# Weights of the first products moved ahead of the norm, one factor ahead of its weights, and output-projection parts placed step by step, in a two-layer decoder trunk

## The chip, the cores and the metric

The kernel runs on one core of a Trainium2 chip. The metric is the device time of one execution in microseconds. The tensor engine (PE) multiplies; the vector engine (DVE), the scalar engine (ACT) and the GpSimd engine (POOL) do the elementwise work; SP and POOL issue the DMA transfers.

## The reference, cut to what matters

The input x has 512 tokens of 1024 features. Two layers follow each other, all in float32:

```
alpha = (2 * DEPTH) ** 0.25
for l in range(2):
    y = mla(x) if l == 0 else swa(x)         # attention of layer A, attention of layer B
    x = layernorm(alpha * x + y)             # the first norm of the layer
    x = layernorm(alpha * x + relu(x @ w_up) ** 2 @ w_down)
```

Layer A's attention has 8 heads of 128 and ends with a product by w_o (1024 x 1024). Layer B's attention has 16 query heads of 64 over 4 shared key and value heads, looks at a window of 128 tokens with a bias per head, and ends with a product by w_so (1024 x 1024). Each MLP goes from 1024 to 4096 features and back.

## The kernel before, in words

**Two halves for one number.** Every float32 operand is split into a high part (a copy on ACT, names wh, xth, oh, fac) and the rest (a subtraction on DVE or POOL, names wl, xtl, ol). A product is three matmuls: high by high, high by low, low by high. The function split emits the ACT copy and then the subtraction. All loads of weights, copies, subtractions and matmuls stand in a program order that the Python code writes; each engine runs its own instructions in that order, and `pinned`, `behind(...)` and `tc.high_priority()` shift single instructions in it.

**Weights as a stream.** All weights form one list, `stream`. Entry i is loaded by SP into one of two raw buffers (or into a buffer of four quarters, wq), and split into a ring of four pairs wh/wl. `weights(name)` hands out the next pair and, while doing so, prepares later entries, at most `AHEAD = 4` on the ring and none at or past `state["hold"]`. The first four entries of each MLP have tiles of their own off the ring ("aside": w_fac, w_quada, w_quadb, w_a). `holds[l]` says how many of them may be prepared before the first norm of layer l, and `prepare(n)` raises that bound by n after each token tile's norm.

**The MLP as seven products.** The 4096 features are worked off in four blocks. Each block's up product is done with seven products of half size (steps U'1 ... U'7) instead of eight, each of two weights of 1024 columns; the down products (D1 ... D7) likewise. The weights of several products are sums of quarters: SP loads the first quarter into wq, it is split, and then a POOL DMA adds the next quarter onto the same buffer (line L191, `accum_op=ALU.add`), which is split in turn, and so on. `XFactors` makes the factors of the input side for the first block. Its method `rest` makes those of products 6, 7 and 4; it is called at the first U'5, before the matmuls of which both weights are taken by `Block.up`.

**The end of the attention and the first norm.** `TokMajor` is the product by w_o or w_so: token tile t (128 tokens) by quarter kp of the contracted features. `part(t, kp)` does 6 matmuls for the left 512 columns. `finish(gb, dst, early)` does the parts not yet done, takes the four weights of the right columns, calls `load_gb` (two loads on SP, L385 and L386, of the norm's g and b), and then for each token tile runs 24 matmuls, the evacuation (L534 on DVE, x = alpha x + mm), the statistics (L527, L531, L393), and the norm itself (L396, rs on POOL at L377, L400). After tile t it prepares `early[t]` more weights: `(0, 2, 1, 2)`. One tile later PE turns the normed tile around by transposes (L623), and ACT and DVE split the result.

**Layer B's attention.** `run_steps` goes over 16 heads: scores of head u + 2 (8 matmuls, then DVE adds the bias, ACT takes the exponential, POOL scales p at L1232 and L1234), filling work, `turn` of head u (transposes of p, L1245 and L1247), and `mix` of head u - 1 (8 matmuls by the values). Every second head ends an o tile, whose split goes to oh on ACT and ol on POOL. Filling work is a list of (cost, latest step, earliest step, function): queries by halves (`queries(m, part)`, 24 matmuls of 512 columns in two parts, whose result ACT and DVE copy to q at L1188 and L1189), values, and six parts of w_so. An entry runs when the cost spent so far is under its share of the total or its latest step has come, and only if its earliest step has come.

Of the kernel before, what the change touches and what calls it, by code (L numbers as in the profile page):

```python
# [48 lines left out]
def build(tc, nc, io, out):  # L49
    with ExitStack() as top:  # L50
# [61 lines left out]
        stream, off_ring = [], []  # L112
# [14 lines left out]
        def queue(name, ap, low=nc.vector):  # L127


            index = len(stream)  # L130

            def make(pieces=1, between=None):
                cols = ap.shape[-1]
                raw = at_hand.pop(index) if index in at_hand else raw_tile()
                wh, wl = tiles_of_weights()
                for j in range(pieces):
                    c = slice(j * cols // pieces, (j + 1) * cols // pieces)
                    if between:
                        between(j)
                    if index not in fetched:  # L140
                        pe(nc.sync.dma_start(raw[:, c], ap[:, c]))
                    split(wh[:, c], wl[:, c], raw[:, c], low)
                return wh, wl

            def fetch(raw):
                at_hand[index] = raw
                fetched.add(index)
                pe(nc.sync.dma_start(raw[:, : ap.shape[-1]], ap))

            fetchers[index] = fetch  # L150
            stream.append((name, make))
            off_ring.append(False)
# [12 lines left out]
        def queue_seven(name, key, chunk):  # L165

            quads = {}

            def half(a, jp):
                if a not in quads:
                    if (key, a) == ("U", "a"):
                        quads[a] = xp.tile([P, 4, 512], F32, tag="xt", bufs=8, name=nm("wq"))
                    elif (key, a) == ("U", "b"):
                        quads[a] = gp.tile([P, 4, 512], F32, tag="gb", bufs=1, name=nm("wq"))
                    else:
                        quads[a] = mlp_pool[0].tile([P, 4, 512], F32, tag="quad" + a, bufs=1, name=nm("wq"))
                return quads[a][:, 2 * jp : 2 * jp + 2, :]

            def flat(ap):
                return ap.rearrange("p a b -> p (a b)")

            def grown(a, jp, *more, aside=None):
                wh, wl = tiles_of_weights(aside)
                with behind(state.get("s4") if (key, a, jp, bool(more)) == ("U", "b", 0, True) else None):
                    state["last"] = split(
                        wh, wl, flat(half(a, jp)), keep=(a, bool(more)) == ("b", True) and key == "U"
                    )
                if more:  # L190
                    nc.gpsimd.dma_start(half(a, jp), chunk(*more, jp), accum_op=ALU.add)  # L191
                return wh, wl

            def loaded(a, jp, at, *more, aside=None):
                pe(nc.sync.dma_start(half(a, jp), chunk(*at, jp)))
                return grown(a, jp, *more, aside=aside)

            def alone(jp, aside=None):
                raw = raw_tile()
                pe(nc.sync.dma_start(raw.rearrange("p (a b) -> p a b", a=2), chunk(1, 0, jp)))  # L200
                wh, wl = tiles_of_weights(aside)
                split(wh, wl, raw)
                return wh, wl

            of = {
                1: lambda jp, aside=None: loaded("a", jp, (0, 0), 0, 1, aside=aside),
                5: lambda jp: grown("a", jp, 1, 1),
                6: lambda jp: grown("a", jp, 1, 0),
                4: lambda jp: grown("a", jp),
                2: alone,  # L210
                3: lambda jp: loaded("b", jp, (1, 1), 0, 1),
                7: lambda jp: grown("b", jp),
            }

            def add(n, asides=(None, None)):
                for jp, aside in enumerate(asides):
                    make = (lambda jp=jp, aside=aside: of[n](jp, aside)) if aside else (lambda jp=jp: of[n](jp))
                    stream.append((name, make))
                    off_ring.append(aside is not None)

            return add
# [23 lines left out]
        holds = []  # L245

        def mlp_stream(l):
            holds.append(len(stream) + 1)
            def up(q):

                return lambda r, c, jp: io["up"][
                    l, q * 8 + 4 * c + 2 * jp : q * 8 + 4 * c + 2 * jp + 2, :, r * 512 : (r + 1) * 512
                ].rearrange("c p x -> p c x")

            def down(q):
                return lambda r, c, jp: io["down"][l, q * 8 + 4 * c + 2 * (1 - r) + jp].rearrange(
                    "p (a b) -> p a b", a=2
                )

            add = {("U", q): queue_seven("up", "U", up(q)) for q in range(NFF)}  # L260
            add |= {("D", q): queue_seven("down", "D", down(q)) for q in range(NFF - 1)}
            for i, (which, q, n) in enumerate(steps_of()):
                if i < 2:
                    add[which, q](n, [lambda j=2 * i + jp: aside_of(j) for jp in range(2)])
                else:
                    add[which, q](n)
            for c in range(8):
                queue("down", io["down"][l, (NFF - 1) * 8 + c])
# [14 lines left out]
        state = {"next": 0, "at": 0, "hold": 0}  # L283
# [50 lines left out]
        b = bank()  # L334
# [258 lines left out]
        class XFactors(Factors):  # L593
# [49 lines left out]
            def rest(self):  # L643

                a11, _, a21, a22 = [f32(self.xf[i][:, n]) for i in range(2) for n in range(2)]
                with behind(state["last"]):
                    nc.vector.tensor_sub(self.a, self.a, a11)
                    split(self.part(6, 0), self.part(6, 1), self.a)
                    nc.vector.tensor_sub(self.b, a11, a21)
                    split(self.part(7, 0), self.part(7, 1), self.b)  # L650
                    split(self.part(4, 0), self.part(4, 1), a22)

        def mlp(src, gb, dst, mp):
# [17 lines left out]
            class Block:  # L671
# [16 lines left out]
                    return self.g[name]  # L688

                def up(self, n):  # L690
                    w = [weights("up") for _ in range(2)]
                    if (self.q, n) == (0, 5):
                        src.rest()
                    key = {3: 3}.get(n) or own_bank[n]
                    for j in range(4):

                        b = self.bank(("U", key), j // 2)
                        wh, wl = w[j // 2]
                        for k in range(4):
                            c = slice(j % 2 * 512 + k * P, j % 2 * 512 + (k + 1) * P)  # L700
                            group(
                                b[:, j % 2 * 256 : j % 2 * 256 + 256],
                                three(wh[:, c], wl[:, c], src.part(n, 0)[:, k, :], src.part(n, 1)[:, k, :]),
                                n not in (2, 4) and k == 0 and j % 2 == 0, k == 3, skip_group_check=True,
                            )
                        if j % 2:
                            self.up_out(n, j // 2)
                        if (self.q, j) == (0, 1) and n in (1, 2):
                            with tc.high_priority():
                                src.turn(n + 1)  # L710
# [74 lines left out]
            at = {}  # L785
# [19 lines left out]
            gb = gb()  # L805
# [320 lines left out]
        with tc.tile_pool(name="mlp0", bufs=1) as mp:  # L1126
            mlp_pool[0] = mp
            state["hold"] = holds[0]
            x1 = XFactors(mp)
            proj.finish(gb, x1, (0, 2, 1, 2))  # L1130
            mlp(x1, lambda: load_gb(io["ln_mlp_g"][0], io["ln_mlp_b"][0]), x2, mp)

        mlp_pool[0] = None
# [1 line left out]
        with tc.tile_pool(name="swa", bufs=1) as mp:  # L1135
# [145 lines left out]
            for m in range(1, 8):  # L1281
                for part in range(2):
                    fill.append((2.6, 2 * m - AHEAD_B - 3 + part, -9, lambda m=m, part=part: queries(m, part)))
                if m == 1:
                    for t in range(1, NT):
                        fill.append((2.6, 0, -9, lambda t=t: values(t)))
            for t in range(2):
                for kp in range(3):
                    at = 11 if (t, kp) < (0, 2) else (11, 14)[t] + kp
                    fill.append((1.3, 11 if at == 11 else 99, at, lambda t=t, kp=kp: proj.part(t, kp)))  # L1290
            load_bias(0)
            begin(
                x2,
# [7 lines left out]
        with tc.tile_pool(name="mlp1", bufs=1) as mp:  # L1301
            mlp_pool[0] = mp
            state["hold"] = holds[1]
            x3 = XFactors(mp)
            proj.finish(gb, x3, (0, 2, 1, 2))
            mlp(x3, lambda: load_gb(io["ln_mlp_g"][1], io["ln_mlp_b"][1]), None, mp)


# [107 lines left out]
```

## Time and profile before

| | us |
|---|---|
| three runs | 1029.98, 1026.42, 1027.87 |
| median | 1027.87 |
| the profiled execution | 1029.26 |
| its span in the profile | 1027.2 |
| mean granted clock of TensorE over the span | 0.99 |

In the profile's rows a start is counted in microseconds from the beginning of the span, and 2.06 us of the profiled execution lie outside it. The engines' rows show for each instruction its start, its duration, its engine, line, operation and tiles, and in brackets how long the engine sat idle before it and what ended the wait. Matmuls are pipelined, so a matmul's duration (0.39 us at 512 columns) is longer than the step to the next one (0.23 us).

### The profile page before, as it was taken

Reading aid. Unit: us, or ns where it says so; the run is one execution under the profiler, and the core shown is the slowest. Engines: PE = TensorE matmul, PEld = TensorE weight load, DVE = VectorE, ACT = ScalarE, POOL = GpSimd, SP = SyncE. Lnnn points to the kernel's source line nnn. Section 1 sums busy time; section 2 is a strip of 40 time slices with the busy share of each in tenths; the row PEclk is TensorE's granted clock in tenths of the full one; section 3 lists DMA queues with packets and bytes.
Section 4 is the critical chain, followed back from the end, with each engine's and each line's share of the span. In section 5 each row is a group of like instructions: output and inputs, shape, how many; then the busy total and the mean of one; then the engine's idle time right before and its main releaser. Section 6 shows DMA issues by size and latency. Waiting matters only on the chain.

```text
span 1027.2 us, 15878 instructions
## 1 busy us (share of the span) xinstructions
PE 1000.3 (97%) x6148; PEld 897.7 (87%) x6148; DVE 768.4 (75%) x1233; ACT 556.4 (54%) x849; POOL 219.1 (21%) x204
## 2 busy tenths in 40 slices
PE   8999999998999999999999998999899999999997
PEld 7888887997999989998889897889799998998986
DVE  5588856988769769886685578498886796797756
ACT  5456643457537637646146689345664664565620
POOL 0231101212211211210004675112022122122000
PEclk9999999999999999999999999999899999999999
DMA  7431126488877986964132212349777788898432
GB/s 241 142 96 42 62 103 185 105 187 226 157 168 209 184 179 195 229 113 144 62 103 93 83 63 73 104 101 224 199 149 152 181 224 149 202 249 154 92 122 82
DMA packets 60246, 149.55 MB, mean 146 GB/s; under 512 B 5211, under 2 KB 9740, under 8 KB 60172
## 3 DMA queue, kind: packets, MB, share of 16 engines
q0 software_dynamic: 24320, 58.73, 32.0%
q1 hardware_dynamic: 35852, 89.82, 25.8%
q8 instruction: 48, 0.79, 0.3%
q14 instruction: 26, 0.21, 0.1%
HBM read 146.41 MB, written 4.22 MB: 147 GB/s over the span
## 4 chain that ended last, share of the span: by engine, by line
PE 85%; DMA 5%; DVE 4%; ACT 3%; issue 1%; SPq 0%; POOL 0%; DVEq 0%; ACTq 0%; POOLq 0%
PE mm L104 78%; PE tr L104 4%; DMA wq<-in_up 3%; DVE wl L80 1%; ACT wh L77 1%; DMA xraw<-in_xT 1%; DMA gb<-in_ln_mix_b 1%; PE tr L1075 1%; DMA raw<-in_w_o 1%; PE tr L1245 1%; DMA raw<-in_w_v 1%; PE tr L623 1%; ACT a L740 0%; PE tr L1247 0%; DVE x L400 0%
## 5 line engine op out<-in xcount | busy, mean ns | idle before, releaser
L104 PE MATMUL mm<-wh,fac 128*128 128x512 f32 (+1 forms) x944 | 295.6, 390 | 6.4 <-ACT fac L77 4.4
L77 ACT ACTIVATE wh<-wq 128x1024 fp32r<-128x1024 f32 x164 | 173.7, 1060 | 207.4 <-PE mm L104 144.0
L80 DVE TENSOR_TENSOR wl<-wq,wh 128x1024 fp32r<-128x1024 f32 x164 | 199.5, 1221 | 81.1 <-ACT wh L77 80.1
L104 PE MATMUL mm<-xth,wh 128*128 128x256 f32 (+1 forms) x936 | 245.7, 290 | 0.2 <-DVE a L734 0.2
L104 PE MATMUL mm<-xth,wl 128*128 128x256 f32 (+1 forms) x808 | 235.3, 291 | 0.0
L104 PEld LDWEIGHTS mm<-wh,fac 128*128 128x128 f32 x944 | 177.4, 189 | 44.0 <-ACT fac L77 4.8
L104 PE MATMUL mm<-xtl,wh 128*128 128x256 f32 (+1 forms) x680 | 199.6, 293 | 1.2 <-DVE xtl L80 1.2
L104 PE MATMUL mm<-wl,fac 128*128 128x512 f32 (+1 forms) x472 | 183.3, 388 | 0.0
L104 PEld LDWEIGHTS mm<-xth,wh 128*128 128x128 f32 x936 | 170.8, 192 | 3.2 <-issue 0.4
L104 PEld LDWEIGHTS mm<-xth,wl 128*128 128x128 f32 x808 | 155.5, 192 | 2.3
L191 POOL DMA_DIRECT2D wq<-in_up x64 | 77.5, 1223 | 279.6 <-DVE wl L80 205.9
L77 ACT ACTIVATE wh<-raw 128x1024 fp32r<-128x1024 f32 (+4 forms) x85 | 84.8, 998 | 92.7 <-PE mm L104 57.6
L104 PEld LDWEIGHTS mm<-xtl,wh 128*128 128x128 f32 x680 | 131.0, 193 | 4.4 <-DVE xtl L80 1.4
L80 DVE TENSOR_TENSOR wl<-raw,wh 128x1024 fp32r<-128x1024 f32 (+3 forms) x64 | 74.9, 1177 | 48.0 <-ACT wh L77 47.8
L104 PEld LDWEIGHTS mm<-wl,fac 128*128 128x128 f32 x472 | 89.5, 190 | 17.0
L191 POOL DMA_DIRECT2D wq<-in_down x48 | 42.0, 876 | 189.9 <-DVE wl L80 170.0
L80 POOL TENSOR_TENSOR wl<-raw,wh 128x1024 fp32r<-128x1024 f32 (+2 forms) x21 | 43.8, 2090 | 81.2 <-ACT wh L77 81.1
L104 PE MATMUL mm<-wh,ol 128*128 128x512 f32 x128 | 50.9, 398 | 1.8 <-POOL ol L80 1.8
L104 PE MATMUL mm<-wl,oh 128*128 128x512 f32 x128 | 50.6, 396 | 1.0 <-DVE wl L80 0.9
L104 PE MATMUL mm<-wh,oh 128*128 128x512 f32 x128 | 51.4, 402 | 0.2 <-ACT oh L77 0.2
L377 POOL TENSOR_TENSOR rs<-mv,half 128x1 f32<-128x1 f32 x16 | 11.1, 691 | 169.4 <-DVE mv L393 169.4
L537 DVE TENSOR_TENSOR x<-mm,x 128x512 f32<-128x512 f32 (+1 forms) x49 | 32.9, 674 | 14.7 <-PE mm L104 14.6
(217 smaller groups left out, 1845.9 us busy)
## 6 DMA issues: line engine op xcount, KB each, us to landing
wq<-in_up POOLq DMA_DIRECT2D x64, 512.0 KB, 7.7
wq<-in_down POOLq DMA_DIRECT2D x48, 512.0 KB, 6.4
wq<-in_up SPq DMA_DIRECT2D x32, 512.0 KB, 5.3
raw<-in_down SPq DMA_DIRECT2D x28, 512.0 KB, 6.8
wq<-in_down SPq DMA_DIRECT2D x24, 512.0 KB, 7.0
raw<-in_up SPq DMA_DIRECT2D x16, 512.0 KB, 5.6
raw<-in_w_o SPq DMA_DIRECT2D x8, 512.0 KB, 3.8
raw<-in_w_sq SPq DMA_DIRECT2D x8, 512.0 KB, 3.3
```

Of the source, the lines that this page charges most:

```text
L77: high = nc.scalar.activation(dst_h, src, AF.Copy)
L80: low = (engine or nc.vector).tensor_sub(dst_l, src, f32(dst_h))
L104: pe(nc.tensor.matmul(dst, st, mv, start=first and i == 0, stop=last and i == len(pairs) - 1, **kw))
L191: nc.gpsimd.dma_start(half(a, jp), chunk(*more, jp), accum_op=ALU.add)
L377: nc.gpsimd.tensor_tensor(r, v, half, ALU.pow)
L537: nc.vector.tensor_add(xs[t][:, c], b, xs[t][:, c])
L623: pe(nc.tensor.transpose(pt[:, a, :], xs[t][:, k * P : (k + 1) * P], ident))
L1075: pe(nc.tensor.transpose(pt[:, kb * P : (kb + 1) * P], p[:, kb * P : (kb + 1) * P], ident))
L1245: pe(nc.tensor.transpose(pt[:, a, 0:P], p[:, kb, P:256], ident))
```

## The change

Four edits. First, `holds` rises by three, and `early` becomes (0, 0, 0, 2): all four weights kept aside are loaded and split before the first norm, and the loads of g and b come behind theirs on SP. The plain splits of the ring note themselves in `state["plain"]`, and the first split of a weight kept aside is placed behind the last of them. Second, `rest()` is called between the two weights of the first U'5 and no longer after them, and the splits of product 6's second weights and the like are placed behind the instructions that make the factor (`state["s2", jp]`). Third, the six filling entries of w_so become eight, cost nothing in the pacing, and each has one step at which it runs. Fourth, since these entries count no cost, the total that paces the other filling work falls from 52.0 to 44.2.

On every engine the number of instructions stays the same, and so does the number of DMA issues; only their order changes.

```diff
-                    split(wh[:, c], wl[:, c], raw[:, c], low)
+                    state["plain"] = split(wh[:, c], wl[:, c], raw[:, c], low)
...
             def grown(a, jp, *more, aside=None):
                 wh, wl = tiles_of_weights(aside)
-                with behind(state.get("s4") if (key, a, jp, bool(more)) == ("U", "b", 0, True) else None):
+                after = None
+                if aside:
+                    after = state.pop("plain", None)
+                elif (key, a, jp, bool(more)) == ("U", "b", 0, True):
+                    after = state.get("s4")
+                elif (key, a, more) == ("U", "a", (1, 0)):
+                    after = state.pop(("s2", jp), None)
+                with behind(after):
                     state["last"] = split(
...
         def mlp_stream(l):
-            holds.append(len(stream) + 1)
+            holds.append(len(stream) + 4)
...
                 with behind(state["last"]):
-                    nc.vector.tensor_sub(self.a, self.a, a11)
-                    split(self.part(6, 0), self.part(6, 1), self.a)
+                    state["s2", 0] = (nc.vector.tensor_sub(self.a, self.a, a11),)
+                    state["s2", 1] = split(self.part(6, 0), self.part(6, 1), self.a)
...
                 def up(self, n):
-                    w = [weights("up") for _ in range(2)]
+                    w = [weights("up")]
                     if (self.q, n) == (0, 5):
                         src.rest()
+                    w.append(weights("up"))
...
-            proj.finish(gb, x1, (0, 2, 1, 2))
+            proj.finish(gb, x1, (0, 0, 0, 2))
...
-            for t in range(2):
-                for kp in range(3):
-                    at = 11 if (t, kp) < (0, 2) else (11, 14)[t] + kp
-                    fill.append((1.3, 11 if at == 11 else 99, at, lambda t=t, kp=kp: proj.part(t, kp)))
+            for t, kp, u in ((0, 0, 11), (0, 1, 11), (1, 0, 13), (1, 1, 14), (2, 0, 14), (2, 1, 15), (0, 2, 15), (1, 2, 16)):
+                fill.append((0, u, u, lambda t=t, kp=kp: proj.part(t, kp)))
...
-            proj.finish(gb, x3, (0, 2, 1, 2))
+            proj.finish(gb, x3, (0, 0, 0, 2))
```

## The prediction

> **What bounds the kernel now.** I read the page's busy times and chain first, then PE's waits, then the granted clock in stretches, then the timelines of the places that the change touches.
>
> ```profile
> PE 1000.3 (97%) x6148; PEld 897.7 (87%) x6148; DVE 768.4 (75%) x1233; ACT 556.4 (54%) x849; POOL 219.1 (21%) x204
> PE 85%; DMA 5%; DVE 4%; ACT 3%; issue 1%; SPq 0%; POOL 0%; DVEq 0%; ACTq 0%; POOLq 0%
> ```
>
> PE works for 97% of the span and carries 85% of the chain. The work on PE stays the same, so the time can only change by the places where PE waits, old ones that go and new ones that come. The old ones, from PE's waits:
>
> ```profile
> PE mm L104 <- ACT fac L77: 4.4, 2, 2.4
> PE tr L104 <- DVE xtl L80: 2.1, 2, 1.1
> PE mm L104 <- POOL ol L80: 1.8, 1, 1.8
> ```
>
> None is over 2.4 us. But a wait can cost twice, because the granted clock halves after some of them. In the stretches the columns are PE, PEld, DVE, ACT and POOL busy, then the clock:
>
> ```profile
> 214.71:218.12 3.41, 1.50 (x11) 1.10 (x9) 3.10 (x3) 2.80 (x4) 0.99 (x1) 1.00 1.13 207
> 218.12:221.54 3.42, 3.42 (x17) 3.42 (x18) 3.33 (x3) 2.90 (x4) 0.21 (x1) 0.50 1.13 206
> 235.19:238.60 3.41, 1.75 (x15) 1.55 (x13) 2.49 (x3) 3.41 (x4) 0.00 (x0) 1.00 1.05 211
> 238.60:242.01 3.41, 2.36 (x9) 1.66 (x10) 2.97 (x4) 3.24 (x4) 0.00 (x0) 1.00 0.77 210
> 637.96:641.37 3.41, 1.65 (x7) 0.73 (x6) 2.21 (x7) 3.36 (x13) 2.88 (x3) 1.00 0.01 2
> 641.37:644.79 3.42, 3.19 (x8) 2.41 (x9) 0.34 (x2) 0.30 (x3) 2.00 (x3) 0.50 0.00 0
> ```
>
> A stretch of 3.41 us with PE busy for 1.50 or 1.65 us is followed by one at clock 0.50; with 1.75 us busy it is not. So about half a stretch idle (1.71 us) halves the next stretch, which then does 1.7 us less work. Whether a wait falls into one stretch or is divided between two depends on where the stretches lie.
>
> A rule speaks to this. The Trainium skill, "TensorE: Matmul & The Clock Gate", section "Why this matters for your kernels", sees a drop only from idle gaps of about 3 us or more, and "What's actually happening" there has the window free-running at 3413 ns. By it no wait of this kernel, old or new, would halve the clock; the rows disagree (0.50 after waits of 2.3 us in sum), and they decide. The length of the window agrees with the rows.
>
> **Part 1, the weights ahead of the norm, layer A.** DVE, PE, ACT and SP at this place:
>
> ```profile
> 167.53 1.23 DVE L80 TENSOR_TENSOR w_fac<-wq,w_fac 128x1024 fp32r<-128x1024 f32 x1 [1.13 <-ACT w_fac L77]
> 169.93 1.22 DVE L80 TENSOR_TENSOR wl<-raw,wh 128x1024 fp32r<-128x1024 f32 x1
> 172.68 0.69 DVE L534 SCALAR_TENSOR_TENSOR x<-x,mm 128x512 f32<-128x512 f32 x1 [0.76 <-PE mm L104]
> 176.12 1.28 DVE L400 SCALAR_TENSOR_TENSOR x<-x,rs,gb 128x1024 f32<-128x1024 f32 x1 [0.46 <-POOL rs L377]
> 169.87 0.39 PE L104 MATMUL mm<-wh,oh 128*128 128x512 f32 x1
> 171.20 0.50 PE L104 MATMUL mm<-wl,oh 128*128 128x512 f32 x1 [0.94 <-DVE wl L80]
> 177.95 0.60 PE L623 MATMUL tr<-ident,x 128*128 128x128 f32 x4
> 167.40 1.04 ACT L77 ACTIVATE wh<-raw 128x1024 fp32r<-128x1024 f32 x1
> 176.83 1.06 ACT L77 ACTIVATE w_a<-raw 128x1024 fp32r<-128x1024 f32 x1 [3.41 <-DMA raw<-in_up]
> raw<-in_w_o SPq DMA_DIRECT2D x1, 512.0 KB, 3.2
> raw<-in_up SPq DMA_DIRECT2D x1, 512.0 KB, 7.8
> ```
>
> *Removed:* the eighth weight of w_o no longer stands behind w_fac on ACT and DVE. Its ACT copy moves from 167.40 to about 165.9, when the matmuls have freed its ring place, and its DVE half from 169.93 to 167.6. PE's wait for it, 171.20 less 169.87 less a step of 0.23, is 1.10 us, and goes. PE then reaches the first transpose (L623) at 176.85, not 177.95.
>
> *Added, on DVE's queue ahead of the evacuation of tile 0 (172.68):* from wl's end at 168.8 come the statistics of the last tile (about 0.7), then w_fac, w_quada and w_quadb at 1.2 each, to 173.1, and then w_a. The last one binds. Its raw buffer is free only when wl has ended, so SP issues its load at 168.8, and the loads of g and b queue behind that. I take 3.9 us to landing, bounded by 3.2 (a weight load that ran alone) and 7.8 (one that stood behind the loads of g and b, which now come later); nearer to 3.2, since the loads of g and b are no longer ahead. It lands at 172.7; ACT's copy ends at 173.75, DVE's part at 174.9. From evacuation to normed tile take 172.68 to 177.40, 4.7 us: the tile is ready at 179.65. PE stands from 176.85 to 179.7, 2.85 us, net 1.75 more than before. With the load at 3.2 DVE itself binds at 173.1 and the net is 1.1; with 5.6, about halfway, it is 3.4. Behind w_a on ACT nothing is due before tile 0's transposes; behind it on DVE waits tile 0's evacuation, and for that PE. The later tiles move with it and lose w_quada, w_quadb and w_a out of their own stretch. POOL issues its second accumulating load ahead of tile 0's rs now, at about 172.9, and is free before rs is due at 176.6. The loads of g and b, issued at 169.3 and 169.7 instead of 161, are needed at 176.7 and 178.4, 7.4 and 8.7 us later; they are covered at the price of a load in a row, and if not, the tile is late by the same amount.
>
> **Part 2, the sixth factor ahead of its weights,** and what it meets next:
>
> ```profile
> 215.44 0.28 PE L104 MATMUL mm<-xth,wl 128*128 128x256 f32 x1
> 216.57 0.38 PE L104 MATMUL tr<-xth,wh 128*128 128x256 f32 x1 [0.84 <-ACT xth L77]
> 218.02 0.51 PE L104 MATMUL tr<-xtl,wh 128*128 128x256 f32 x1 [1.07 <-DVE xtl L80]
> 715.93 0.39 PE L104 MATMUL tr<-xtl,wh 128*128 128x256 f32 x1 [1.07 <-DVE xtl L80]
> 236.66 0.28 PE L104 MATMUL mm<-xth,wl 128*128 128x256 f32 x1
> 238.93 0.50 PE L104 MATMUL mm<-wh,fac 128*128 128x512 f32 x1 [1.99 <-ACT fac L77]
> 736.20 0.50 PE L104 MATMUL mm<-wh,fac 128*128 128x512 f32 x1 [2.44 <-ACT fac L77]
> ```
>
> The waits are 1.00 + 1.33 = 2.33 us in layer A and 1.33 in layer B (start to start less a step of 0.12). The factor's halves are moved past one weight split, some 1.1 us on ACT and 1.2 on DVE (rows of w_a and wl above), and PE itself comes 1.75 us later out of part 1, while the factor's inputs do not. That is 2.9 us or more against 2.33, so the waits go; without the delay of part 1 about 1.1 us would stay in layer A. What is late next is the first D'1, 238.93. There ACT has a row of copies and squares ahead of fac, fed by the products just before (it is busy for all of 235.19 to 238.60 above). If PE arrives a little earlier, this queue moves with it only as far as the weights' accumulated loads allow. I keep the wait: about 0.2 us of the gain is given back in layer A, and 0.5 us gained in layer B. Ends: nothing given back, or all 2.33.
>
> Layer A so far: -1.10 + 2.85 - 2.33 + 0.2 = -0.4 us.
>
> **Part 3, the filling work of layer B.** The total cost falls from 52.0 to 44.2, so each step's target falls by 15%, and one early entry slips by a step: the 24 matmuls of a value part (128x256) that stood between the scores of head 1 and of head 2 come after both.
>
> ```profile
> 555.71 0.28 PE L104 MATMUL mm<-skl,q 128*128 128x256 f32 x1
> 555.83 0.28 PE L104 MATMUL mm<-wh,xth 128*128 128x256 f32 x1
> 556.96 0.68 DVE L1189 TENSOR_TENSOR q<-mm,q 64x512 fp32r<-64x512 f32 x1
> ```
>
> Head 2's q ends on DVE at 557.64. Before, PE had 24 x 0.12 = 2.9 us of value work from 555.83 on to cover it. Now the scores of head 2, and all PE work behind them, wait: PE stands from 555.83 to 557.69: +1.86 us. The value work comes later and hides nothing, because PE has no later wait nearby. Bounds: 0 if DVE takes q ahead of head 1's bias additions (about 1.4 us of it), 1.9 if not; the order has q behind them, so 1.86.
>
> At the end of the attention:
>
> ```profile
> 634.94 0.38 PE L104 MATMUL mm<-skh,q 128*128 128x256 f32 x1 [0.43 <-DVE o L1275]
> 636.33 0.20 ACT L1225 ACTIVATION_READ_ACCUMULATOR p<-mm,nb 128x1 f32 x1
> 638.85 1.47 POOL L1234 TENSOR_TENSOR p<-p,ri 128x768 f32<-128x768 f32 x1
> 640.28 1.27 POOL L80 TENSOR_TENSOR ol<-o,oh 128x512 fp32r<-128x512 f32 x1
> 641.60 0.80 PE L104 MATMUL mm<-wh,ol 128*128 128x512 f32 x1 [1.80 <-POOL ol L80]
> ```
>
> Between 634.94 and 641.60 PE stands for about 3 us in sum, start to start less the steps; the largest piece is that for ol (1.80 and the restart), which POOL could begin only after a p of 1.47 us. The parts of w_so now lie between the transposes and mixes, and ol is split ahead of that p: these waits go. One comes: the first part that is moved needs a bank that head 14's scores free only when ACT has taken their exponential, at 636.53; PE gets there when the four score steps from 634.94 are done, at about 635.45, and waits about 1.1 us. Net -2.0 us; ends -3.1 (the bank is free) and -1.0.
>
> **Part 4, the front of the norm in layer B.**
>
> ```profile
> 668.81 1.21 DVE L80 TENSOR_TENSOR wl<-raw,wh 128x1024 fp32r<-128x1024 f32 x1
> 674.64 1.28 DVE L400 SCALAR_TENSOR_TENSOR x<-x,rs,gb 128x1024 f32<-128x1024 f32 x1
> 676.79 1.03 PE L623 MATMUL tr<-ident,x 128*128 128x128 f32 x8
> ```
>
> Here the normed tile was ready at 675.92, 0.87 us early, and PE hardly waited for wl (about 0.2). By the sum of part 1 the same edit puts w_a's end 6.0 us behind wl's end, and the tile 10.4 us behind it instead of 5.9: 4.5 later. wl itself comes earlier against PE, as w_fac's ACT copy (1.06) and DVE half (1.23) no longer stand ahead of it; evacuations still do, and I take 1.4 of at most 2.3. So PE waits 4.5 - 0.87 - 1.4 = 2.2 to 2.4, and with the wait for wl gone the net is +2.1 (0.8 with wl at its earliest and the load at 3.2; 4 with the load at 5.6).
>
> Layer B: 1.86 - 2.0 + 2.1 - 1.33 - 0.5 = +0.1 us. Both layers: **-0.3 us** at full clock.
>
> **The clock.** Of the halved stretches the one at 218.12 goes (-1.7), and that at 641.37 with a chance of two thirds (-1.1), as 1.7 us of wait is left there. New waits can halve: a wait of w falls into one stretch with 1.71 us or more at about w/3.41 of the positions. That is 0.85 for 2.85 us, 0.55 for 1.86, 0.7 for 2.35, and some 0.7 for the first D'1 of layer A, which was just above the limit (1.75) and waits a little longer at first. Together 2.8 stretches, 4.8 us. The sum is -0.3 - 2.8 + 4.8 = +1.7 us: 1031.0 against the profiled execution (1029.26). That one lies 1.4 above the median of the runs, and the runs are spread over 3.6 us, two halved stretches; against the median the same sum gives 1029.5. A difference of 0.3%, 3.1 us, is about what a measurement of this kernel can tell from no change.
>
> **The rivals.** (a) *Every new wait halves the clock* and the tail's stays: 4 x 1.7 - 1.7 - 0.3 = +4.8, 1032.7. For it: the rows of 1.50 and 1.65; against it: 1.75 did not. It decides from 1.71 us of idle time in one stretch. (b) *w_a lands late,* 5.6 us after its issue: 1.7 more in each layer, 1.7 + 3.4 = +5.1, 1033.0. For it: the other loads in the same row took 7.8; against: two of those loads now come behind. (c) *The change of part 2 does not do what it says:* the accumulated loads of the weights around it set the pace there, and a wait for them takes the place of that for xth: 3.7 us of gain absent, +5.4, 1033.3. Against it: the rows name xth and xtl, not a weight. (d) *The front waits stay short and halve nothing*: load at 3.2 (-0.7 per layer), 218.12 and 641.37 both at full clock: -0.3 - 1.4 - 3.4 = -5.1, 1022.8. (e) *The new waits halve nothing, and none of the old halved stretches goes:* -0.3, 1027.6. For it: 1.75 us busy did not halve; against it: 1.50 and 1.65 did. The rule of the Trainium skill on the clock gate, named above, leads to this case.
>
> **How the numbers follow.** The forecast 0.47, (a) 0.23, (b) 0.08, (c) 0.06, (d) 0.12, (e) 0.04. The forecast and (e) fall mostly within 0.3%, (a) to (c) and a little of the forecast are slower, (d) and a little faster: 0.14, 0.48, 0.38. The range runs from 1024.5, the middle of the way to (d), to 1033.5, which holds (a) to (c).
>
> **What would show it.** After: no wait for wl near 170; a PE wait of some 2.9 us ahead of the first L623 of layer A, released by L400 with w_a's split ahead of the evacuation; no wait for xth or xtl at U'6; a wait of some 1.9 us for q in the early heads; no wait for ol; 2.3 us ahead of L623 in layer B. It is wrong if those front waits are under 1 us, if the q wait is absent, or if the clock keeps 1.00 behind them.

## The result, and the profile after

| | kernel before | changed kernel |
|---|---|---|
| median of 16 runs each | 1028.21 us | 1031.45 us |
| fastest and slowest of them | 1022.62, 1032.43 | 1028.02, 1035.40 |
| ratio | 1 | 1.0039, 95% interval 1.0021 to 1.0057 |
| span of the profiled execution | 1027.2 us | 1030.4 us |

The changed kernel is slower by 0.39%, between 0.2 and 0.6%. The prediction had +1.7 us as its forecast, 1029.5 against the median of three runs that it knew (1027.87), and a range of 1024.5 to 1033.5.

The page's busy times of the changed kernel, its chain, and then PE's waits (in all, how often, the longest). L407 here is L400 of before, L630 is L623, L742 is L734, L1197 is L1189, L1233 is L1225.

```profile
PE 998.7 (97%) x6148; PEld 897.6 (87%) x6148; DVE 769.6 (75%) x1233; ACT 556.3 (54%) x849; POOL 218.5 (21%) x204
PE 82%; DMA 6%; DVE 5%; ACT 3%; issue 3%; POOL 0%; SPq 0%; DVEq 0%; ACTq 0%; POOLq 0%
```

```profile
PE tr L630 <- DVE x L407: 5.9, 2, 3.1
PE mm L104 <- ACT fac L77: 4.9, 2, 2.4
PE mm L104 <- DVE a L742: 2.1, 2, 1.4
PE mm L104 <- ACT p L1233: 2.0, 2, 1.1
PE mm L104 <- DVE q L1197: 1.7, 1, 1.7
```

The work is the same, and PE's share of the chain has gone from 85% to 82%. PE is busy for 998.7 us instead of 1000.3, in a span that is 3.2 us longer: it stands idle for 31.7 us instead of 26.9. So the loss is waiting. The waits for xth and xtl at U'6, for ol and for wl are gone. In their place stand the waits for the normed tile (5.9 us in two places), for q (1.7), for p (2.0) and, twice, for a (2.1). None of these four was in the table of before with more than 0.2 us. The wait for fac was there and has grown by 0.5.

Where it happened in layer A, on SP, ACT, DVE and PE (start, duration, and in brackets the idle time before):

```profile
164.13 4.60 SPq L207 DMA_DIRECT2D raw<-in_up  x2
169.18 0.34 SPq L392 DMA_DIRECT2D gb<-in_ln_mix_g  x1
167.13 1.22 DVE L80 TENSOR_TENSOR wl<-raw,wh 128x1024 fp32r<-128x1024 f32 x1
172.47 1.06 ACT L77 ACTIVATE w_a<-raw 128x1024 fp32r<-128x1024 f32 x1 [1.71 <-DMA raw<-in_up]
173.56 1.22 DVE L80 TENSOR_TENSOR w_a<-raw,w_a 128x1024 fp32r<-128x1024 f32 x1 [1.04 <-ACT w_a L77]
174.70 0.68 DVE L541 SCALAR_TENSOR_TENSOR x<-x,mm 128x512 f32<-128x512 f32 x1
177.81 1.28 DVE L407 SCALAR_TENSOR_TENSOR x<-x,rs,gb 128x1024 f32<-128x1024 f32 x1
179.15 1.09 PE L630 MATMUL tr<-ident,x 128*128 128x128 f32 x8 [2.72 <-DVE x L407]
```

The eighth weight's wl ends at 168.35; only then does SP issue the second raw load, and the loads of g and b behind it. The raw load lands 4.1 us after its issue, and ACT begins w_a at 172.47. DVE splits w_a at 173.56 and only then takes up tile 0, whose norm ends at 179.09. PE stood for 2.72 us in the bracket. In layer B, and at the two places where PE now waits for a:

```profile
666.37 1.21 DVE L80 TENSOR_TENSOR wl<-raw,wh 128x1024 fp32r<-128x1024 f32 x1
672.90 1.23 DVE L80 TENSOR_TENSOR w_a<-raw,w_a 128x1024 fp32r<-128x1024 f32 x1 [1.14 <-ACT w_a L77]
677.47 1.28 DVE L407 SCALAR_TENSOR_TENSOR x<-x,rs,gb 128x1024 f32<-128x1024 f32 x1 [0.46 <-POOL rs L384]
678.81 1.97 PE L630 MATMUL tr<-ident,x 128*128 128x128 f32 x8 [3.14 <-DVE x L407]
230.76 0.47 PE L104 MATMUL mm<-xth,wh 128*128 128x256 f32 x2 [0.63 <-DVE a L742]
731.11 0.47 PE L104 MATMUL mm<-xth,wh 128*128 128x256 f32 x2 [1.42 <-DVE a L742]
239.18 0.50 PE L104 MATMUL mm<-wh,fac 128*128 128x512 f32 x1 [2.44 <-ACT fac L77]
```

In layer B's attention, the wait for q, one for p that was not foreseen, and the end:

```profile
554.95 0.28 PE L104 MATMUL mm<-skl,q 128*128 128x256 f32 x1
556.93 0.33 PE L104 MATMUL mm<-skh,q 128*128 128x128 f32 x1 [1.70 <-DVE q L1197]
594.24 1.06 ACT L77 ACTIVATE wh<-raw 128x1024 fp32r<-128x1024 f32 x1 [2.22 <-DMA raw<-in_w_so]
596.77 0.50 PE L104 MATMUL mm<-xth,wh 128*128 128x512 f32 x1 [1.08 <-ACT p L1233]
639.27 0.49 PE L104 MATMUL mm<-wh,oh 128*128 128x512 f32 x1 [0.91 <-ACT p L1233]
```

The clock, in stretches (PE, PEld, DVE, ACT and POOL busy, then the granted clock), cut where the clock changes. First three of before, then the changed kernel:

```profile
535.56:538.97 3.41, 3.41 (x16) 3.41 (x17) 1.79 (x4) 0.38 (x1) 0.00 (x0) 0.50 0.00 0
736.94:740.36 3.42, 2.71 (x6) 2.15 (x7) 2.99 (x3) 2.16 (x3) 0.00 (x0) 0.50 0.71 229
740.36:743.77 3.41, 3.41 (x9) 2.64 (x8) 2.29 (x4) 1.06 (x1) 0.00 (x0) 0.50 0.95 343
```

```profile
176.81:180.22 3.41, 1.07 (x9) 1.07 (x10) 3.27 (x4) 0.38 (x1) 0.20 (x1) 1.00 1.11 202
180.22:183.63 3.41, 3.41 (x10) 2.63 (x9) 3.25 (x6) 1.90 (x4) 0.56 (x1) 0.50 0.03 5
238.25:241.66 3.41, 1.76 (x6) 1.16 (x7) 3.41 (x3) 3.38 (x4) 0.00 (x0) 1.00 0.87 243
241.66:245.07 3.41, 3.41 (x9) 2.64 (x8) 1.85 (x3) 1.51 (x2) 0.00 (x0) 0.50 0.84 222
675.15:678.57 3.42, 0.52 (x3) 0.10 (x1) 2.89 (x4) 0.00 (x0) 1.65 (x1) 1.00 1.13 204
678.57:681.98 3.41, 3.17 (x12) 2.88 (x13) 2.82 (x6) 1.70 (x3) 0.50 (x1) 0.50 0.35 64
740.00:743.42 3.42, 2.81 (x8) 1.97 (x7) 2.99 (x3) 2.42 (x3) 0.00 (x0) 0.50 0.87 283
743.42:746.83 3.41, 3.41 (x10) 2.64 (x9) 2.29 (x4) 1.06 (x1) 0.00 (x0) 0.50 0.88 336
```

The halved stretches of before at 218, 535 and 641 are gone. Three new ones stand behind both fronts (180 and 679) and behind the first D'1 of layer A (242). The two behind the first D'1 of layer B are in both kernels. So each profile has five while PE still works, and their number explains none of the difference. The timed runs say the same: their mean granted clock is 0.9896 over the 16 runs of the changed kernel, and 0.9898 over the 64 runs of the kernel before that were taken beside the experiments.

### The profile page after: what moved, and what is told of

It is laid out like the page before. It is cut to its first block, busy times and chain, and to the rows that moved or that the text cites. A ratio compares the mean times of both kernels' runs of the same rounds, so it can differ in the third digit from the quotient of the medians.

```text
span 1030.4 us, 15886 instructions
## 1 busy us (share of the span) xinstructions
PE 998.7 (97%) x6148; PEld 897.6 (87%) x6148; DVE 769.6 (75%) x1233; ACT 556.3 (54%) x849; POOL 218.5 (21%) x204
## 4 chain that ended last, share of the span: by engine, by line
PE 82%; DMA 6%; DVE 5%; ACT 3%; issue 3%; POOL 0%; SPq 0%; DVEq 0%; ACTq 0%; POOLq 0%
PE mm L104 75%; PE tr L104 4%; DMA wq<-in_up 3%; ACT wh L77 1%; DMA raw<-in_w_o 1%; DMA raw<-in_up 1%; DVE wl L80 1%; PE tr L1083 1%; DMA raw<-in_w_so 1%; PE tr L630 1%; PE tr L1253 1%; DVE x L403 0%; DMA raw<-in_w_kv 0%; DVE bn L534 0%; DVE x L407 0%
```

## The experiments

All kernels are compared with the kernel before by timed runs on the same chip. Each ratio is to the kernel before; differences against the changed kernel go over its 1.0039 and are only as good as the two intervals. The last column is the mean granted clock of the timed runs, and behind it that of the kernel before in the same measurement.

| run | median us | ratio to before | 95% interval | mean clock (before) |
|---|---|---|---|---|
| part 1 alone | 1031.84 | 1.0044 | 1.0026 to 1.0062 | 0.9899 (0.9901) |
| part 2 alone | 1024.32 | 0.9974 | 0.9956 to 0.9992 | 0.9918 (0.9901) |
| part 3 alone | 1030.08 | 1.0029 | 1.0010 to 1.0048 | 0.9884 (0.9901) |
| part 3, pacing kept | 1025.14 | 0.9973 | 0.9958 to 0.9989 | 0.9913 (0.9901) |
| all, w_a behind tile 1's norm | 1022.83 | 0.9954 | 0.9931 to 0.9977 | 0.9929 (0.9895) |
| all, two weights behind tile 1's norm | 1022.01 | 0.9938 | 0.9916 to 0.9960 | 0.9915 (0.9895) |
| the same, pacing kept | 1018.67 | 0.9900 | 0.9877 to 0.9924 | 0.9925 (0.9895) |
| all, front filled with matmuls | 1029.04 | 1.0005 | 0.9987 to 1.0022 | 0.9921 (0.9895) |
| all, g and b loaded first | 1034.51 | 1.0060 | 1.0040 to 1.0080 | 0.9885 (0.9893) |
| two weights, pacing kept, D'1 filled | 1016.71 | 0.9892 | 0.9873 to 0.9911 | 0.9970 (0.9893) |

By an estimate from the span (some 1026 us), a mean clock lower by 0.001 costs about 1 us, if PE has work throughout the halved time. The differences of the mean clock are uncertain by 0.001 to 0.0025.

My theory was the prediction's sum: the fronts and the wait for q cost what parts 2 and 3 gain, and halved stretches come on top. The rivals: that everything ahead of the accumulated loads is given back at D'1, so that only part 3 counts; that the late loads of g and b, not w_a, make the front; that the w_so parts themselves, not the fallen total, make the wait for q; that the clock has nothing to do with these waits.

**Part 1 alone.** The edits of parts 2 and 3 are undone:

```diff
-                    w = [weights("up")]
+                    w = [weights("up") for _ in range(2)]
                     if (self.q, n) == (0, 5):
                         src.rest()
-                    w.append(weights("up"))
...
+                    fill.append((1.3, 11 if at == 11 else 99, at, lambda t=t, kp=kp: proj.part(t, kp)))
```

> Part 1 alone (all four weights ahead of the first norm, loads of g and b behind theirs; the sixth factor and layer B's filling work as before). Theory of the prediction: the wait for wl near 170 (1.1 us) goes; ahead of the first transposes of the normed tile PE waits 2.9 us in layer A and about 2.9 us in layer B, where the attention's end is as late as before; the waits at U'6 go by themselves, because PE comes later. Without the clock +0.2 us, with 0.5 to 1.5 more halved stretches +1 to +3 us. Rival (all time lost or won ahead of the accumulated loads is made up at the first D'1): PE's place after D'1 of layer A is within 0.5 us of that of the kernel before, time within 0.1%.

It is slower by 0.44% with the mean clock of before, so this part carries the loss, and it does so by waiting, where the expectation had +0.2 us without the clock. PE's waits for the normed tile:

```profile
PE tr L630 <- DVE x L407: 7.6, 2, 4.4
```

One is 3.2 us in layer A, as expected, but the other is 4.4 in layer B, half again what I had. PE reaches the first D'1 of layer A at 238.70, within 0.5 us of the kernel before (238.93), as the rival had it, but that of layer B at 742.17 instead of 736.20. So in this profile the loss lies between the two, and the rival's time within 0.1% falls.

**Part 2 alone.** `holds`, `early` and the filling work as before; only `rest()` and the splits behind it are moved.

```diff
-            holds.append(len(stream) + 4)
+            holds.append(len(stream) + 1)
...
-            proj.finish(gb, x1, (0, 0, 0, 2))
+            proj.finish(gb, x1, (0, 2, 1, 2))
```

> Part 2 alone (the sixth factor ahead of its second weights). Theory of the prediction: the waits for xth and xtl at U'6 (2.3 us in layer A, 1.3 in layer B) go or shrink to about 1 us, and the time falls by 1 to 3 us. Rival (the accumulated loads around it set the pace): the waits for xth and xtl go, but PE waits as long a little later, for a (U'7's result, L742 in the changed kernel), some 2 us in layer A and 1.8 us in layer B, and the time stays within 0.1%.

```profile
PE mm L104 <- DVE a L742: 3.4, 2, 1.8
```

The waits for xth and xtl at U'6 are gone, and PE waits for a instead, 1.6 and 1.8 us: the rival has the mechanism. Yet the time is 0.26% lower, which the rival does not have and the path does not explain (2.9 us of bracketed waiting at U'6, 2.1 for xtl and 0.8 for xth, became 3.4 behind U'7). The runs' clock explains most of it: 0.9918 instead of 0.9901, by the estimate above 1.8 us of some 2.7. The difference of the clocks is uncertain by as much as itself (0.0017), and why fewer stretches are halved stays open.

**Part 3 alone, and with the pacing kept.** The second differs from the first by one number:

```diff
-                fill.append((0, u, u, lambda t=t, kp=kp: proj.part(t, kp)))
+                fill.append((0.975, u, u, lambda t=t, kp=kp: proj.part(t, kp)))
```

> Part 3 alone (eight parts of w_so at fixed steps, without cost). Theory of the prediction: a wait of 1.9 us for q near 555, a second one of about 1.2 us near 595 as in the changed kernel, no wait for ol at the end of the attention, where 3 us of waits become 1.7; in sum +1 us without the clock, +0.5 to +3 with it. Rival (the wait at the end of the attention was the only one that counts): -2 us.

> Part 3 alone, but each of the eight entries costs 0.975, so that the total that paces the other filling work is 52.0 as before. Theory (the fallen total made the waits near 555 and 595): both are absent, the waits at the end of the attention are as in part 3, and the time is 1.5 to 2 us under the kernel before, 2 to 4 us under part 3 alone. Rival (the waits near 555 and 595 come from the w_so parts themselves): they stay, and so does the time of part 3.

Part 3 alone is 0.29% slower and, with the total kept at 52.0, 0.27% faster, 0.56% apart. The wait for q is in the first and not in the second; the end of the attention is the same in both. In the first:

```profile
PE mm L104 <- DVE q L1196: 1.7, 1, 1.7
PE mm L104 <- ACT p L1232: 0.9, 1, 0.9
```

So the fallen total makes it, not the w_so parts. By the estimate above about 3 of the 4.9 us between the two medians lie in the clock (0.9884 against 0.9913), the rest is the wait itself. The second expected wait, near 595, did not come in either: in the changed kernel's profile ACT stood for a weight's transfer there (2.22 us). None of the other kernels with these fixed steps shows it, so it belongs to that execution.

**The front: which weight binds.** Two kernels move weights back behind tile 1's norm, a third moves the loads of g and b ahead again:

```diff
-            holds.append(len(stream) + 4)
+            holds.append(len(stream) + 3)    # the second kernel: + 2
...
-            proj.finish(gb, x1, (0, 0, 0, 2))
+            proj.finish(gb, x1, (0, 1, 0, 2))    # the second kernel: (0, 2, 0, 2)
```

```diff
-                    ws = [weights(self.name) for _ in range(4)]
                     if callable(gb):
                         gb = gb()
+                    ws = [weights(self.name) for _ in range(4)]
```

> The changed kernel with w_a's first pair entry kept for after the norm of tile 1: the bound before the first norm is three of the four weights, early is (0, 1, 0, 2). Theory (w_a, whose load waits for a raw buffer and so for wl, binds the evacuation of tile 0): the evacuation starts where w_quadb ends, the wait ahead of the first transposes falls from 2.9 to about 1.0 us in layer A and from 3.3 to about 0.7 in layer B, no halved stretch follows either, and the time is 3 to 7 us under the changed kernel. Rival (the loads of g and b, which stand behind the second raw load on SP, make the norm late): the wait falls too, but DVE then sits idle ahead of the norm's own operations on g and b instead of ahead of w_a.

> The changed kernel with only two of the four weights (the w_fac and w_quada entries) ahead of the first norm and the others behind the norm of tile 1, early (0, 2, 0, 2). Theory (each split of 1.2 us on DVE ahead of tile 0's evacuation is paid by PE): no wait ahead of the first transposes in either layer, no wait for wl near 170, 5 to 8 us under the changed kernel. Rival (what is gained at the front is given back at the first D'1): the front waits go, but PE's place after D'1 stays that of the changed kernel within 0.5 us in layer A.

> The changed kernel with the loads of g and b issued ahead of the weights of the norm's front, as they stood before the change. Theory (w_a's load, which waits for wl, binds the front, and each transfer ahead of it delays it): the wait ahead of the first transposes grows from 2.9 to about 4 us in layer A and from 3.3 to 4 or more in layer B; 1 to 3 us slower than the changed kernel. Rival (late loads of g and b make the front): the wait falls by the time that the norm's operations waited for them, and the kernel is faster than the changed one.

PE's wait for the normed tile, with w_a moved back, and with g and b first:

```profile
PE tr L630 <- DVE x L407: 1.3, 2, 0.8
```

```profile
PE tr L630 <- DVE x L407: 6.8, 2, 3.4
```

Moving one weight takes the two waits from 5.9 to 1.3 us in sum and the time from 1.0039 to 0.9954. With two moved the row is absent, and the time is 0.9938, not to be told from the first. PE reaches the first D'1 of layer A at 235.27 and 237.27 instead of 239.18, so what is won at the front is not given back there, and that rival falls. With g and b first, their loads cannot be late, and the waits grow to 6.8 us, 3.4 in each layer, less than the 4 that I expected: DVE waits 1.02 us for w_a again, and later.

```profile
175.19 1.22 DVE L80 TENSOR_TENSOR w_a<-raw,w_a 128x1024 fp32r<-128x1024 f32 x1 [1.02 <-ACT w_a L77]
```

The rival of late g and b falls.

**The clock.** In the changed kernel nine more matmuls of 512 columns stand behind tile 1's group; their bank is overwritten.

```diff
+                            if early and t == 1:
+                                spare = bank()
+                                group(spare, [(self.src.h(0, slice(0, P)), ws[0][0][:, 0:512])] * 9)
```

> The changed kernel with nine matmuls of 512 columns more behind tile 1's group, ahead of the first transposes of each layer; they write a bank whose next group starts afresh, so nothing they compute is used. They fill 2.0 us of the wait of 2.9 and 3.3 us. Theory (about half a stretch idle halves the next): the remaining waits of 0.9 and 1.3 us are followed by no halved stretch, and the time falls by 1.5 to 3.5 us although PE does more. Rival (the clock follows only idle gaps of 3 us and more, or something else than the waits): the halved stretches behind the fronts stay where they are or come at random, and the time is that of the changed kernel within 0.1%.

Stretches around the two fronts, columns as above:

```profile
176.90:180.30 3.40, 3.25 (x15) 2.36 (x13) 3.23 (x4) 0.00 (x0) 0.56 (x1) 1.00 1.12 204
180.30:183.70 3.40, 3.08 (x18) 2.70 (x19) 3.31 (x7) 2.05 (x4) 0.55 (x1) 1.00 0.57 104
675.70:679.10 3.40, 3.26 (x15) 2.37 (x13) 3.19 (x5) 0.00 (x0) 0.56 (x1) 1.00 1.09 197
679.10:682.50 3.40, 3.00 (x17) 2.63 (x18) 3.31 (x7) 1.97 (x4) 0.55 (x1) 1.00 0.61 111
```

The clock stays at 1.00 behind both fronts, where it was 0.50, and the ratio is 1.0005 against 1.0039, about 3.5 us (2.4 us by the medians), although PE does more. The two intervals touch (1.0022 and 1.0021), so the time alone would not settle it. The mean clock of the runs does more: 0.9921 against 0.9896, a difference of 0.0025 that is uncertain by 0.0014, worth about 2.6 us by the estimate above. The profile by itself shows only the two places, for five stretches are halved in it too, one of them behind the wait for q.

A wait of this length need not halve anything. In the profile of part 1 alone PE waited 3.20 us ahead of the transposes of layer A (179.43), and the wait is divided between two stretches. PE is busy for 1.81 us of each, and none of the three rows is halved:

```profile
174.42:177.83 3.41, 1.81 (x8) 1.15 (x7) 3.10 (x5) 0.00 (x0) 1.43 (x1) 1.00 1.05 197
177.83:181.24 3.41, 1.81 (x12) 1.68 (x13) 3.06 (x4) 1.08 (x2) 0.23 (x1) 1.00 0.75 137
181.24:184.66 3.42, 3.42 (x16) 2.80 (x16) 3.32 (x5) 1.20 (x2) 0.55 (x1) 1.00 0.00 0
```

**The version that beats both.** Two weights ahead of the norm, two behind tile 1's, part 2 as it is, and part 3 at 0.975:

> Two of the four weights ahead of the first norm as in the run before, and the filling entries of w_so at 0.975 each, so that the total is 52.0 again. Theory: the wait for q near 555 goes as well, another 1.9 us and up to one halved stretch; in sum 7 to 10 us under the changed kernel and 4 to 8 us under the kernel before. Rival (halved stretches appear wherever some wait is left, so that the time is kept): within 0.3% of the kernel before.

Its waits for the normed tile and for q are gone. Among what is left of PE's waits, in the MLPs:

```profile
PE mm L104 <- ACT fac L77: 4.9, 2, 2.4
PE mm L104 <- DVE a L742: 1.1, 1, 1.1
```

It runs 1.0% faster than the kernel before (0.76 to 1.23%), and about 1.4% faster than the changed one. Of the 9 us against the kernel before about 3 lie in the clock by the estimate above. The last kernel also fills the wait at the first D'1:

```diff
+                        if (self.q, n, t) == (0, 1, 0):
+                            group(b[:, 0:256], [(src.part(4, 0)[:, 0, 0:P], src.part(4, 0)[:, 0, :])] * 16)
```

> Two of the four weights ahead of the first norm, the filling work paced as before, and sixteen matmuls of 256 columns more ahead of the first D'1 of each layer, into the bank that D'1's first group then starts afresh, so that nothing they compute is used. They fill 1.9 us of PE's wait for fac (2.6 us). Theory (about half a stretch idle halves the next): no halved stretch behind D'1 in either layer, where the two-weights kernel has one or two in each, and 2 to 5 us under that kernel. Rival (the copies on ACT and DVE set the time there, and halved stretches merely replace waiting): the halved stretches go and the time stays within 0.1% of the two-weights kernel.

Stretches around the first D'1, without and with the filling:

```profile
233.50:236.90 3.40, 0.97 (x6) 0.50 (x4) 2.48 (x4) 3.40 (x4) 0.00 (x0) 1.00 1.00 187
236.90:240.30 3.40, 2.68 (x7) 2.03 (x7) 2.97 (x3) 2.34 (x3) 0.00 (x0) 0.51 0.71 224
```

```profile
232.00:235.50 3.50, 3.50 (x32) 3.50 (x31) 2.03 (x3) 3.50 (x5) 0.41 (x1) 1.00 1.05 205
235.50:239.00 3.50, 2.27 (x10) 1.46 (x10) 3.39 (x3) 3.47 (x4) 0.00 (x0) 1.00 0.80 216
```

The halved stretches go, and the runs' clock rises from 0.9925 to 0.9970, by the estimate 4.6 us if PE had work throughout. Yet the time of 0.9892 against 0.9900 is not told from no gain, and 2 to 5 us less was expected. So most of what the clock gave back did not shorten the path: this is what the rival says, that the copies set the time there and halved stretches replace waiting. Whether that is all of it, or 1 us or so is gained, stays open.

## Why the prediction was right or wrong

The direction and the range held, but the sum came near by luck. It had -0.3 us at full clock and +2.0 us from the clock (4.8 - 2.8). Measured, the clock adds nothing (five halved stretches in each profile, 0.9896 against 0.9898 over the runs), and the 3.2 us of the span are waits at full clock: two errors of opposite sign. The likeliest case (within 0.3%) was on the wrong side of the line by a little, with 0.39% measured, and the interval reaches down to 0.21%. By its steps:

- **Front of layer A: right.** w_a's load took 4.1 us from issue to landing, for 3.9; the normed tile came at 179.09, not 179.65, with everything 0.4 earlier. The bracket is 2.72 us, the wait start to start 2.88, for 2.85. That w_a and not g and b binds is shown by the three front kernels.
- **Front of layer B: mis-sized.** The wait is 3.3 us start to start (3.14 in the bracket), not 2.2 to 2.4. The failing term is the tile 10.4 us behind wl's end: it is 11.2 (667.58 to 678.75). About 0.5 of that is w_a's split, which ends 6.55 us behind wl's end, not 6.0 (DVE waits 1.14 for ACT's copy); the rest lies in the norm, where DVE waits 0.46 for POOL. wl came 1.2 us earlier against PE, for 1.4.
- **Part 2: the waits at U'6 went, as said, but what is late next was missing a place.** I looked for it at the first D'1. It stood already between U'7 and U'4: DVE's a (L742) lies behind the splits of weights that the accumulated loads feed, and PE waited 0.63 and 1.42 us there in brackets. Rival (c), at 0.06, had this mechanism in part. Part 2 alone shows it plainly: 3.4 us. At the first D'1 the wait for fac is 2.44 us in both layers: in layer A 0.45 longer, for 0.2, and in layer B the 0.5 us that were to be gained did not come.
- **The wait for q: right in size** (1.86 us start to start between 554.95 and 556.93, one step off) and in cause, by the kernel with the pacing kept.
- **The end of the attention: right.** The wait for the moved part is 0.91 in the bracket, 1.1 start to start; the wait for ol is gone.
- **The clock: right in its places, wrong in its balance.** The stretches at 218 and 641 went, and new ones came behind both fronts and D'1 of layer A, as taken. But the one at 535, which the sum left out, went too, and the one behind q did not come in this profile. It did come behind the same wait in three other kernels (two weights, front filled, g and b first), so there the place of the stretches decides. The term of +2.0 us came to nothing.
- **The rule behind the clock: near, but too sharp.** 1.76 us busy halved the clock here, where 1.75 us did not in the kernel before. In other profiles 1.56 us did not (w_a moved back, from 726.65 on) and 2.08 us did (two weights, from 635.13 on), so the profile's busy time gives no sharp limit. The rule that only gaps of some 3 us do it stays contradicted by the front of layer A (2.72) and its first D'1 (2.44), which halved, and by the divided 3.20 us of part 1 alone, which did not; the front of layer B (3.14) agrees with it.
- **The sum.** Part 1 (+0.44%), part 2 (-0.26%) and part 3 (+0.29%) add up to +0.47%, against +0.39% together. What the sum at full clock lacked is the waits for a (2.1 us), the wait near 595 (1.1, of one execution), the front of layer B (1.0) and the two D'1 (0.75), together some 4.9 us; the clock's 2.0 stands against it. That would make 4.6 us for a span longer by 3.2. Of the difference, 0.4 us was there ahead of the first front; the rest I can't place.

## What to carry to other kernels

A weight that is prepared earlier takes its place in every queue it passes: here a split of 1.2 us on DVE ahead of the norm was paid by PE once its load, which waited for a buffer, came last. Move only as many as fit into the time that is idle ahead of the waiting instruction; with the other edits the same, two of the four ahead of the norm make the kernel 0.6% faster than before, all four 0.4% slower. In a list of work paced by costs, taking the cost away from some entries moves all others too: keep the total when only the places are meant to change. And a forecast that adds waits to halved stretches is checked part by part, idle time by the page and the clock by the runs: here the total agreed, and both parts were wrong.

## What the runs showed of the hardware

Nine matmuls of no use, 2.0 us of work put into a wait, took the halved clock away behind both fronts (0.50 to 1.00), raised the mean clock of the runs from 0.9896 to 0.9921, and took 2.4 us off the median. Filling the wait at D'1 in the same way took the halved stretches away too (0.9925 to 0.9970), with no gain that could be told from the spread of the runs. A wait of 2.72 us within one stretch of 3.41 us was followed by a halved one; a wait of 3.20 us divided between two was not.
